# Up-projection of an MLP as seven half-size block products, and the layer's first half run for all tokens ahead of it

## The chip, the cores and the metric

The kernel runs on one core of a Trainium2 chip. The metric is the device time of one execution in microseconds (us). The kernel before has a median of 2953.45 us in 3 runs (2952.11 to 2954.23).

The engines, by the names that the profile uses: PE is TensorE (matmuls; PEld its weight loads), DVE is VectorE, ACT is ScalarE, POOL is GpSimd, SP is SyncE, whose queue issues all of this kernel's data transfers. SBUF is the on-chip memory of 128 partitions; PSUM holds the matmul results in 8 banks of 128x512 float32.

## The reference, cut to what matters

One decoder layer on 2048 tokens of width 1024, float32. What stands ahead of the last part (attention of two kinds, gates, merge) is not touched by the change and gives `mix`, 2048 x 1024. Then:

```python
x = x + mix @ w_out                                  # output projection, 1024 x 1024
h2 = rmsnorm(x, ln2_g)                               # second norm
x = x + jnp.square(jax.nn.relu(h2 @ w_up)) @ w_down  # MLP, 1024 -> 4096 -> 1024
```

## The kernel before, in words

**Precision.** Matmuls are in a reduced float32 form (`fp32r`). So every operand is split into a high part (a cast on ScalarE, line 91) and a low part (source minus high part, a subtraction on VectorE or GpSimd, line 92), and every product is three matmuls, high x high, high x low, low x high, that add up in one PSUM bank (`mm3`, lines 94 to 98). Here "a matmul" is one of these: a 128x128 stationary piece against 512 columns.

**Stages.** Attention and gates first, up to about 1353 us; they write `mix` to DRAM. Then the tokens go in two halves of 1024, `hf` = 0 and 1 (line 824), and each half passes two stages:

- Output projection, 8 blocks `i` of 128 tokens. `load_mix` loads and splits a block of `mix` and loads the same rows of x into a tile `x2[i]`; 2 x 8 products of 3 matmuls with w_out (all 16 pieces `wo` are in SBUF, in the pool "w") give `po`, which VectorE adds to `x2[i]`. Then the second norm: `norm2_pre` (a sum of squares on ScalarE, two small steps on GpSimd, a scaling `hn` on VectorE, line 758), and `norm2_post` (8 transposes `h2ps` on TensorE, a multiplication by the gain, and the split into `h2`, which stays in SBUF). `norm2_post` of a block is written behind the matmuls of the next one; that of the last block of a half behind the first unit of the MLP (line 849).
- MLP, 16 blocks `f` of 256 hidden columns. The weights of a block are loaded into the buffers `raw` (three of 4 KB a partition for all of the kernel) and split by ScalarE and GpSimd (`mlp_weights`). The up part: for two groups `c` of 512 tokens and two pieces `m` of 128 hidden columns, `up_unit` does 8 products, 24 matmuls, into one bank `pup`, then relu on ScalarE (line 820), times itself on VectorE (line 821), and the split into `u`. The down part: for 8 blocks of tokens and two halves of the width, 6 matmuls into a bank `pd`, which VectorE adds to `x2[i]` (line 860). After the last block the rows go out.

**What sets the order.** The text above is in the order in which the program writes it. The library puts it into another one at build time (`schedule_with_timeline_sim=True`, line 882): a planner takes instructions by their place in the text, but lets a later one go first on an engine where the earlier one is not ready by the planner's own estimate, or finds no free buffer. Each engine, and SP's queue of transfers, then runs its own list strictly in that order. A tile named with a `tag` takes one of `bufs` buffers, and waits for one where all are in use.

Of the kernel before, what the change touches and what calls it, by code (L numbers as in the profile page):

```python
# [43 lines left out]
RIGHT = "right"  # L44
# [15 lines left out]
def hybrid_layer(tc, x, positions, ln1_g, w_in, q_norm_a, k_norm_a, q_norm_b, k_norm_b, sinks,  # L60
                 w_branch_a, w_branch_b, w_out, ln2_g, w_up, w_down, out):
    nc = tc.nc
    x, out = x[0], out[0]
    positions = positions[0]
    w_in, w_branch_a, w_branch_b = w_in[0], w_branch_a[0], w_branch_b[0]
    w_out, w_up, w_down = w_out[0], w_up[0], w_down[0]

    const = tc.alloc_tile_pool(name="const", bufs=1)
    rawp = tc.alloc_tile_pool(name="rawp", bufs=3)
# [4 lines left out]
    edge = tc.alloc_tile_pool(name="edge", bufs=1, side=RIGHT)  # L74
# [19 lines left out]
    def mm3(out, lhs, rhs, first, last):  # L94

        nc.tensor.matmul(out, lhs[0], rhs[0], start=first, stop=False)  # L96
        nc.tensor.matmul(out, lhs[0], rhs[1], start=False, stop=False)  # L97
        nc.tensor.matmul(out, lhs[1], rhs[0], start=False, stop=last)  # L98


    ident = const.tile([P, P], F32, name="ident")
# [484 lines left out]
    pools = {}  # L586
# [5 lines left out]
    def B4(name, dtype=F32R):  # L592
        return pools["B"].tile([P, D], dtype, tag="B", bufs=19, name=name)

    def tmp(name, dtype=F32, shape=(P, 512)):
        return pools["A"].tile(list(shape), dtype, tag="tmp", bufs=4, name=name)

    def wslot(name):
        return pools["w"].tile([P, D], F32R, tag="w", bufs=16, name=name)

    def split_raw(name, r, n=D, eng=None):

        hi, lo = wslot(name + "h"), wslot(name + "l")
        split(hi[:, 0:n], lo[:, 0:n], r[:, 0:n], eng)
        return hi, lo
# [51 lines left out]
    for t in range(NBL + 5):  # L657
        if 0 < t < NBL - 1:
            a_split(t + 1)
        if t < NBL:  # L660
            a_project(t)
            g, n = blocks[t]
# [43 lines left out]
        m = t - (3 * NB + 5)  # L706
# [38 lines left out]
                    load_os(c + 2, i2)  # L745


    up_src = w_up.rearrange("(k p) n -> p k n", p=P)
    MF = FC // P
    NF = DFF // FC  # L750
    x2, h2, hn = {}, {}, {}
    mpool = pools["A"]

    def norm2_pre(i):
        xt = x2[i]
        rs = rms_scale(xt, tmp(f"junky{i}", BF16, (P, D)), mpool, i, "y")
        hn[i] = B4(f"hn{i}", F32)
        nc.vector.tensor_scalar(hn[i], xt, rs, None, op0=ALU.mult)

    def norm2_post(i):  # L760
        c = i // 4
        if i % 4 == 0:
            al = [[A4 if c % 2 == 0 or k2 == 0 else B4 for k2 in range(4)] for e in range(2)]
            h2[c] = [[al[e][k2](f"h2{e}_{c}_{k2}").rearrange("p (k t) -> p k t", k=2) for k2 in range(4)]
                     for e in range(2)]
        xt = hn.pop(i)
        pts = []
        for half in range(2):
            pt = bank(f"h2ps{i}_{half}")
            for j in range(4):  # L770
                k = 4 * half + j
                nc.tensor.transpose(pt[:, j * P:(j + 1) * P], xt[:, k * P:(k + 1) * P], ident)
            pts.append(pt)
        for half, pt in enumerate(pts):
# [4 lines left out]
            for k2 in range(2):  # L779
                hi, lo = [h2[c][e][2 * half + k2][:, :, (i % 4) * P:(i % 4 + 1) * P] for e in range(2)]  # L780
                split(hi, lo, t2[:, 2 * k2:2 * k2 + 2, :])

    def out_weights(hf):
        res = []
        for k in range(KD):
            r = raw(f"rwo{hf}_{k}")
            nc.sync.dma_start(r, w_out[k * P:(k + 1) * P, :])
            res.append(split_raw(f"wo{hf}_{k}", r, eng=nc.gpsimd if k % 2 else nc.vector))
        return res

    def mlp_weights(hf, f):
        wu, wd = [], []
        for m in range(MF):
            c0 = f * FC + m * P
            r = raw(f"rwu{hf}_{f}_{m}")
            nc.sync.dma_start(r.rearrange("p (k n) -> p k n", k=KD), up_src[:, :, c0:c0 + P])
            w = split_raw(f"wu{hf}_{f}_{m}", r, eng=nc.gpsimd)
            wu.append([[w_[:, k * P:(k + 1) * P] for w_ in w] for k in range(KD)])
        for m in range(MF):
            c0 = f * FC + m * P  # L800
            r = raw(f"rwd{hf}_{f}_{m}")
            nc.sync.dma_start(r, w_down[c0:c0 + P, :])
            wd.append(split_raw(f"wd{hf}_{f}_{m}", r, eng=nc.gpsimd))
        return wu, wd

    def load_mix(i):
        r = raw(f"rmix{i}")
        nc.sync.dma_start(r.rearrange("p (k t) -> p k t", k=KD), mix_dram[:, :, i * P:(i + 1) * P])
        mx = B4(f"mh{i}"), B4(f"ml{i}")
        split(mx[0], mx[1], r)  # L810
        x2[i] = B4(f"x2_{i}", F32)
        nc.sync.dma_start(x2[i], x[i * P:(i + 1) * P, :])
        return mx

    def up_unit(f, c, m, wu, us):
        pu = bank(f"pup{f}_{c}_{m}")
        for k in range(KD):
            mm3(pu, wu[m][k], [h2[c][e][k // 2][:, k % 2, :] for e in range(2)], k == 0, k == KD - 1)
        r = tmp(f"relu{f}_{c}_{m}")
        nc.scalar.activation(r, pu, AF.Relu)  # L820
        nc.vector.tensor_tensor(r, r, pu, op=ALU.mult)  # L821
        split(us[0][:, m * 512:(m + 1) * 512], us[1][:, m * 512:(m + 1) * 512], r)

    for hf in range(2):
        wo = out_weights(hf)
        mx = load_mix(8 * hf)
        for i in range(8 * hf, 8 * hf + 8):
            nxt = load_mix(i + 1) if i % 8 < 7 else None
            for nh in range(2):
                ns = slice(nh * 512, (nh + 1) * 512)  # L830
                po = bank(f"po{i}_{nh}")
                for k in range(KD):
                    ks = slice(k * P, (k + 1) * P)
                    mm3(po, [t[:, ks] for t in mx], [t[:, ns] for t in wo[k]], k == 0, k == KD - 1)
                nc.vector.tensor_tensor(x2[i][:, ns], x2[i][:, ns], po, op=ALU.add)
            if i % 8 > 0:
                norm2_post(i - 1)
            norm2_pre(i)
            mx = nxt
        w_next = mlp_weights(hf, 0)  # L840
        for f in range(NF):
            wu, wd = w_next
            us = {}
            for c in (2 * hf, 2 * hf + 1):
                us[c] = [B4(f"u{e}_{f}_{c}") for e in "hl"]
                for m in range(MF):
                    up_unit(f, c, m, wu, us[c])
                    if f == 0 and c % 2 == 0 and m == 0:
                        norm2_post(8 * hf + 7)
                if c == 2 * hf and f + 1 < NF:  # L850
                    w_next = mlp_weights(hf, f + 1)
            for i in range(8 * hf, 8 * hf + 8):
                u = us[i // 4]
                for nh in range(2):
                    ns = slice(nh * 512, (nh + 1) * 512)
                    pd = bank(f"pd{f}_{i}_{nh}")
                    for m in range(MF):
                        t0 = m * 512 + (i % 4) * P
# [4 lines left out]
    for pool in (pools["B"], edge, pools["A"], pools["w"], dram, psp, rawp, const):  # L863
        pool.release()


# [19 lines left out]
```

## Time and profile before

| what | us |
|---|---|
| median of 3 runs | 2953.45 |
| the profiled execution | 2951.59 |
| its span (first to last instruction) | 2949.8 |
| attention and gates, until the first output projection | 1353.9 |
| first half: first up matmul to the second half's first `po` matmul | 1447.3 to 2150.2 |
| second half: first up matmul to the last down matmul | 2243.4 to 2945.6 |

The span is the time from the first to the last instruction on the chip; what lies between it and the time of the execution is start and end. A row of the timeline gives the start, the duration, engine, source line, operation, the tile written and those read, and the count; in brackets how long the engine was idle before it and what ended that. Neighbouring matmuls overlap, so their durations add up to more than the time that passes.

### The profile page before, as it was taken

What the parts mean: (1) busy time and instruction counts of PE and PEld (TensorE: products, weight loads), DVE (VectorE), ACT (ScalarE), POOL (GpSimd) and SP (SyncE); (2) the same over time, 40 slices, a digit from 0 to 9 for tenths busy, and PEclk for the clock granted to TensorE, in tenths of its full rate; (3) what the DMA queues carried; (4) which work ended last, traced back from release to release, by engine and by line L of the source; (5) the groups of instructions that cost most, each with busy time, mean ns of one, the idle gap of its engine ahead of it and who ended that gap; (6) DMA issues with size and microseconds to landing.
All of it is one profiled execution on the core that took longest, in us unless ns stands there. A gap on an engine that the chain in (4) does not pass through costs nothing.

```text
span 2949.8 us, 37614 instructions
## 1 busy us (share of the span) xinstructions
PE 2896.2 (98%) x14665; PEld 2425.5 (82%) x14665; DVE 1415.4 (48%) x2839; ACT 1032.3 (35%) x2123; POOL 956.5 (32%) x832
## 2 busy tenths in 40 slices
PE   7999999999989999999999999999999999999999
PEld 6888888887868888888788888888887888888887
DVE  8776676569983123123543334334445344334334
ACT  5565666667873123112311211212223211211210
POOL 6566666666641102111321221212113221211210
PEclk9999999999999999999999999999999999999999
DMA  5321010011144224223311111111243111111101
GB/s 163 96 83 33 12 55 14 12 57 54 56 123 148 77 78 150 64 74 115 93 54 47 51 50 44 56 44 43 76 146 93 51 50 43 51 50 43 58 22 58
DMA packets 220259, 198.04 MB, mean 67 GB/s; under 512 B 12192, under 2 KB 189360, under 8 KB 220080
## 3 DMA queue, kind: packets, MB, share of 16 engines
q1 hardware_dynamic: 220080, 195.63, 21.6%
q8 instruction: 115, 1.88, 0.3%
q14 instruction: 64, 0.52, 0.1%
HBM read 157.65 MB, written 37.95 MB: 66 GB/s over the span
## 4 chain that ended last, share of the span: by engine, by line
PE 93%; DVE 3%; POOL 1%; ACT 1%; issue 1%; DMA 1%; SPq 0%; POOLq 0%; ACTq 0%; DVEq 0%
PE pd L97 8%; PE pd L98 8%; PE pd L96 8%; PE pup L96 8%; PE pup L97 8%; PE pup L98 8%; PE pg L98 4%; PE pg L96 4%; PE pg L97 4%; PE psA L96 3%; PE psA L98 3%; PE psA L97 3%; PE sp L416 2%; PE pt L461 2%; PE po L96 2%; PE po L97 2%
## 5 line engine op out<-in xcount | busy, mean ns | idle before, releaser
L860 DVE TENSOR_TENSOR x<-x,pd 128x512 f32<-128x512 f32 x512 | 351.4, 687 | 362.3 <-PE pd L98 358.6
L821 DVE TENSOR_TENSOR relu<-relu,pup 128x512 f32<-128x512 f32 x128 | 87.8, 686 | 393.9 <-ACT relu L820 393.9
L92 POOL TENSOR_TENSOR wd_0l<-rwd,wd_0h 128x1024 fp32r<-128x1024 f32 x32 | 76.9, 2402 | 520.5 <-ACT wd_0h L91 520.4
L96 PE MATMUL psA<-wah,hsh 128*128 128x512 f32 x512 | 208.7, 408 | 3.4 <-DVE mx L420 1.5
L97 PE MATMUL psA<-wal,hsh 128*128 128x512 f32 x512 | 202.1, 395 | 5.8 <-DVE wal L92 5.7
L91 ACT CAST wd_0h<-rwd 128x1024 fp32r<-128x1024 f32 x32 | 33.7, 1052 | 491.6 <-PE pd L97 491.6
L98 PE MATMUL psA<-wah,hsl 128*128 128x512 f32 x512 | 201.5, 394 | 1.2 <-DVE hsl L92 1.2
L96 PE MATMUL pup<-h,wu_1h 128*128 128x512 f32 x512 | 200.2, 391 | 0.0
L97 PE MATMUL pup<-h,wu_1h 128*128 128x512 f32 x512 | 199.7, 390 | 0.0
L98 PE MATMUL pup<-h,wu_1l 128*128 128x512 f32 x512 | 199.5, 390 | 0.0
L96 PE MATMUL pup<-h,wu_0h 128*128 128x512 f32 x512 | 199.3, 389 | 0.0
L97 PE MATMUL pup<-h,wu_0h 128*128 128x512 f32 x512 | 199.2, 389 | 0.0
L98 PE MATMUL pup<-h,wu_0l 128*128 128x512 f32 x512 | 199.2, 389 | 0.0
L96 PE MATMUL pd<-wd_0h,uh 128*128 128x512 f32 x512 | 199.2, 389 | 0.0
L97 PE MATMUL pd<-wd_0l,uh 128*128 128x512 f32 x512 | 199.2, 389 | 0.0
L98 PE MATMUL pd<-wd_0h,ul 128*128 128x512 f32 x512 | 199.2, 389 | 0.0
L96 PE MATMUL pd<-wd_1h,uh 128*128 128x512 f32 x512 | 199.2, 389 | 0.0
L97 PE MATMUL pd<-wd_1l,uh 128*128 128x512 f32 x512 | 199.2, 389 | 0.0
L98 PE MATMUL pd<-wd_1h,ul 128*128 128x512 f32 x512 | 199.2, 389 | 0.0
L92 POOL TENSOR_TENSOR wu_0l<-rwu,wu_0h 128x1024 fp32r<-128x1024 f32 x32 | 77.1, 2409 | 344.8 <-ACT wu_0h L91 344.8
L820 ACT ACTIVATE relu<-pup 128x512 f32<-128x512 f32 x128 | 75.7, 591 | 277.1 <-PE pup L98 277.1
L97 PE MATMUL psB<-wal,hsh 128*128 128x256 f32 x512 | 144.9, 283 | 0.0
(458 smaller groups left out, 7207.8 us busy)
## 6 DMA issues: line engine op xcount, KB each, us to landing
rwu<-in_w_up_dram SPq DMA_DIRECT2D x64, 512.0 KB, 3.9
rwd<-in_w_down_dram SPq DMA_DIRECT2D x64, 512.0 KB, 3.6
x<-in_x_dram SPq DMA_DIRECT2D x32, 512.0 KB, 4.6
rg<-in_w_in_dram SPq DMA_DIRECT2D x32, 512.0 KB, 3.7
rw<-in_w_in_dram SPq DMA_DIRECT2D x28, 384.0 KB, 3.5
hT_dram<-hT SPq DMA_DIRECT2D x16, 512.0 KB, 3.9
mix_dram<-sig SPq DMA_DIRECT2D x32, 256.0 KB, 2.0
rwo<-in_w_out_dram SPq DMA_DIRECT2D x16, 512.0 KB, 3.5
```

The costliest lines, as they stand in the source:

```text
L91: nc.scalar.copy(hi, src)
L92: (eng or nc.vector).tensor_tensor(lo, src, hi, op=ALU.subtract)
L96: nc.tensor.matmul(out, lhs[0], rhs[0], start=first, stop=False)
L97: nc.tensor.matmul(out, lhs[0], rhs[1], start=False, stop=False)
L98: nc.tensor.matmul(out, lhs[1], rhs[0], start=False, stop=last)
L416: nc.tensor.matmul(sp[:, e * 256:e * 256 + nk], ring[:, own, q_, :], ring[:, slots, k_, :], start=(i == 0), stop=(i == 1))
L461: nc.tensor.transpose(pt[:, h * P:(h + 1) * P], p[4 * q4 + h][:, kb * P:(kb + 1) * P], ident)
L820: nc.scalar.activation(r, pu, AF.Relu)
L821: nc.vector.tensor_tensor(r, r, pu, op=ALU.mult)
L860: nc.vector.tensor_tensor(x2[i][:, ns], x2[i][:, ns], pd, op=ALU.add)
```

## The change

The up-projection is computed by Strassen's algorithm, in the form of Winograd with seven products. A block of the transposed result, 256 hidden columns x 1024 tokens, is cut in 2 x 2: `A11, A21, A12, A22` are the weights (two halves of 512 input channels, two pieces of 128 hidden columns), `B11 ... B22` the activations (two halves of the input channels, two groups of 512 tokens). Four sums of weight blocks (`S1` to `S4`) and four of activation blocks (`T1` to `T4`) are formed in float32 and split. Then seven products of 4 x 3 matmuls take the place of four units of 8 x 3. In the order of the text, and called P1 to P7 below: A11 B11, S1 T1, S2 T2, A12 B21, S3 T3, A22 T4, S4 B22. Four PSUM banks collect them; P4, P5 and P7 add into a bank that holds an earlier product, after that one has been read. VectorE combines the banks into the four quarters of the result (`c11`, `u3`, `c22`, `u2`) in SBUF.

The order of the stages changes too. The output projection and the second norm now run for all 16 blocks of tokens in one go, w_out is loaded and split once, and x2 and h2 are stored to DRAM. Then the pools of these stages are released, and new ones lie over their space, each tile of which waits for the old tiles at its place (`reuse_waits="tile"`). For each half, `token_operands` loads h2 through the `raw` buffers, four k slices of two loads each, and makes the seven activation operands, which stay in SBUF for the half's 16 blocks (14 tiles of 8 KB; there is one set). `x2` is loaded again. The weight operands of a block have 10 tiles where one block uses 14; the split w_down has 4, one block's worth. The sums of the weights and all their splits are on GpSimd and ScalarE. The scratch area for transfers that GpSimd would issue is cut to 256 bytes.

```diff
-    def up_unit(f, c, m, wu, us):
-        pu = bank(f"pup{f}_{c}_{m}")
-        for k in range(KD):
-            mm3(pu, wu[m][k], [h2[c][e][k // 2][:, k % 2, :] for e in range(2)], k == 0, k == KD - 1)
-        r = tmp(f"relu{f}_{c}_{m}")
-        nc.scalar.activation(r, pu, AF.Relu)
-        nc.vector.tensor_tensor(r, r, pu, op=ALU.mult)
-        split(us[0][:, m * 512:(m + 1) * 512], us[1][:, m * 512:(m + 1) * 512], r)
...
+    mx = load_mix(0)
+    for i in range(NB):
+        nxt = load_mix(i + 1) if i + 1 < NB else None
...
+        nc.sync.dma_start(x2_dram[i * P:(i + 1) * P, :], x2[i])
+        if i > 0:
+            norm2_post(i - 1)
+        norm2_pre(i)
+        mx = nxt
+    norm2_post(NB - 1)
+    for pool in (pools["B"], pools["A"], pools["w"]):
+        pool.release()
...
+    def token_operands(hf):
+
+        ops = {n: [poolT.tile([P, 4, 512], F32R, tag="t", bufs=14, name=f"{n}{e}{hf}") for e in "hl"]
+               for n in B_NAMES}
+        ts = slice(1024 * hf, 1024 * hf + 1024)
+        for k in range(4):
+            r1, r2 = raw(f"rh1_{hf}_{k}"), raw(f"rh2_{hf}_{k}")
+            nc.sync.dma_start(r1, h2_dram[:, k, ts])
+            nc.sync.dma_start(r2, h2_dram[:, k + 4, ts])
+            b11, b12, b21, b22 = r1[:, 0:512], r1[:, 512:1024], r2[:, 0:512], r2[:, 512:1024]
+
+            def put(n, src, eng):
+                split(ops[n][0][:, k, :], ops[n][1][:, k, :], src, eng)
+
+            put("B11", b11, nc.vector)
+            t1, t2 = Ft(f"t1_{hf}_{k}"), Ft(f"t2_{hf}_{k}")
+            nc.gpsimd.tensor_tensor(t1, b12, b11, op=ALU.subtract)
+            put("T1", t1, nc.vector)
+            nc.vector.tensor_tensor(t2, b22, t1, op=ALU.subtract)
+            put("T2", t2, nc.vector)
+            put("B21", b21, nc.gpsimd)
+            t3, t4 = Ft(f"t3_{hf}_{k}"), Ft(f"t4_{hf}_{k}")
+            nc.gpsimd.tensor_tensor(t3, b22, b12, op=ALU.subtract)
+            put("T3", t3, nc.vector)
+            nc.vector.tensor_tensor(t4, b21, t2, op=ALU.subtract)
+            put("T4", t4, nc.vector)
+            put("B22", b22, nc.gpsimd)
+        return ops
+
+    def up_operands(hf, f):
+
+        r = []
+        for h in range(2):
+            r.append(raw(f"rwu{hf}_{f}_{h}").rearrange("p (k n) -> p k n", k=4))
+            nc.sync.dma_start(r[h], up_src[h][:, :, f * FC:(f + 1) * FC])
...
+        def summed(n, a, b, op):
+            t = poolS.tile([P, 4, P], F32, tag="s", bufs=2, name=f"s{n}_{hf}_{f}")
+            nc.gpsimd.tensor_tensor(t, a, b, op=op)
+            return t
...
+        def put(n, src):
+            res[n] = [poolS.tile([P, 4, P], F32R, tag="S", bufs=10, name=f"{n}{e}_{hf}_{f}") for e in "hl"]
+            split(res[n][0], res[n][1], src, nc.gpsimd)
+
+        put("A11", a11)
+        s1 = summed("1", a21, a22, ALU.add)
+        put("S1", s1)
+        s2 = summed("2", s1, a11, ALU.subtract)
+        put("S2", s2)
+        put("A12", a12)
+        s4 = summed("4", a12, s2, ALU.subtract)
+        s3 = summed("3", a11, a21, ALU.subtract)
+        put("S3", s3)
+        put("A22", a22)
+        put("S4", s4)
+        return res
...
+        def done(src, m, c):
+
+            nc.vector.scalar_tensor_tensor(src, src, 0.0, src, op0=ALU.max, op1=ALU.mult)
+            split(us[c][0][:, m * 512:(m + 1) * 512], us[c][1][:, m * 512:(m + 1) * 512], src)
...
+        product(ba, "A11", "B11")
+        nc.scalar.copy(p1, ba)
+        product(bc, "S1", "T1")
+        product(bb, "S2", "T2")
+        nc.vector.tensor_tensor(u2, p1, bb, op=ALU.add)
+        product(ba, "A12", "B21", more=True)
+        c11 = Ft(f"fc11_{tag}")
+        nc.scalar.activation(c11, ba, AF.Relu)
+        nc.vector.tensor_tensor(c11, c11, ba, op=ALU.mult)
+        split(us[0][0][:, 0:512], us[0][1][:, 0:512], c11)
+        product(bb, "S3", "T3", more=True)
+        nc.vector.tensor_tensor(u3, p1, bb, op=ALU.add)
+        nc.vector.tensor_tensor(c22, u3, bc, op=ALU.add)
+        product(bd, "A22", "T4")
+        nc.vector.tensor_tensor(u3, u3, bd, op=ALU.add)
+        done(u3, 1, 0)
+        done(c22, 1, 1)
+        product(bc, "S4", "B22", more=True)
+        nc.vector.tensor_tensor(u2, u2, bc, op=ALU.add)
+        done(u2, 0, 1)
+        return us
 
     for hf in range(2):
...
+        A_next = up_operands(hf, 0)
+        B = token_operands(hf)
+        for j in range(8):
+            i = 8 * hf + j
+            x2[i] = poolX.tile([P, D], F32, tag="x2", bufs=8, name=f"x2m_{i}")
+            nc.sync.dma_start(x2[i], x2_dram[i * P:(i + 1) * P, :])
         for f in range(NF):
...
+            A = A_next
+            us = up_products(hf, f, A, B)
+            wd = down_operands(hf, f)
+            if f + 1 < NF:
+                A_next = up_operands(hf, f + 1)
```

## Rows read from the trace of the kernel before

**Rows 1.** The page's first part: busy us, share of the span, instructions.

```profile
span 2949.8 us, 37614 instructions
PE 2896.2 (98%) x14665; PEld 2425.5 (82%) x14665; DVE 1415.4 (48%) x2839; ACT 1032.3 (35%) x2123; POOL 956.5 (32%) x832
```

**Rows 2.** TensorE's waits from 1340 us on: us in total, times, longest.

```profile
PE h2ps L772 <- DVE hn L758: 7.3, 2, 3.7
```

**Rows 3.** Windows, one MLP block: PE, PEld, DVE, ACT, POOL, clock, DMA, GB/s.

```profile
1600.00:1643.52 43.52, 43.52 (x193) 36.05 (x192) 16.79 (x24) 8.77 (x12) 9.56 (x4) 1.00 0.16 49
```

**Rows 4.** The page's groups: busy us, mean ns of one, idle before.

```profile
L96 PE MATMUL pd<-wd_0h,uh 128*128 128x512 f32 x512 | 199.2, 389 | 0.0
```

**Rows 5.** TensorE's timeline within an up part: start us, duration us.

```profile
1600.71 0.39 PE L96 MATMUL pup<-h,wu_1h 128*128 128x512 f32 x1
1600.93 0.39 PE L97 MATMUL pup<-h,wu_1h 128*128 128x512 f32 x1
```

**Rows 6.** TensorE's timeline at the handovers and at the end.

```profile
1447.33 0.48 PE L96 MATMUL pup<-h,wu_0h 128*128 128x512 f32 x1
...
1456.68 1.91 PE L772 MATMUL h2ps<-ident,hn 128*128 128x128 f32 x8 [3.65 <-DVE hn L758]
1458.24 0.78 PE L96 MATMUL pup<-h,wu_1h 128*128 128x512 f32 x1
1458.82 0.63 PE L97 MATMUL pup<-h,wu_1h 128*128 128x512 f32 x1
...
2150.15 0.39 PE L96 MATMUL po<-wo_0h,mh 128*128 128x512 f32 x1
...
2243.36 0.48 PE L96 MATMUL pup<-h,wu_0h 128*128 128x512 f32 x1
...
2945.64 0.39 PE L98 MATMUL pd<-wd_1h,ul 128*128 128x512 f32 x1
```

**Rows 7.** Windows, after TensorE's wait in the first handover; the clock is 0.73.

```profile
1457.00:1463.00 6.00, 6.00 (x25) 5.12 (x24) 5.28 (x5) 3.76 (x7) 5.95 (x3) 0.73 0.61 188
```

**Rows 8.** Groups by form in the MLP, the last from the page.

```profile
L860 DVE TENSOR_TENSOR x<-x,pd 128x512 f32<-128x512 f32 x512 | 351.4, 687 | 362.3 <-PE pd L98 358.6
L92 DVE TENSOR_TENSOR ul<-relu,uh 128x512 fp32r<-128x512 f32 x128 | 104.8, 819 | 64.6 <-ACT uh L91 64.6
...
L91 ACT CAST uh<-relu 128x512 fp32r<-128x512 f32 x128 | 79.5, 621 | 115.2 <-DVE relu L821 115.2
...
L92 POOL TENSOR_TENSOR wd_0l<-rwd,wd_0h 128x1024 fp32r<-128x1024 f32 x32 | 76.9, 2402 | 520.5 <-ACT wd_0h L91 520.4
```

**Rows 9.** Timelines of VectorE and GpSimd, alone and side by side.

```profile
1597.53 0.69 DVE L92 TENSOR_TENSOR ul<-relu,uh 128x512 fp32r<-128x512 f32 x1 [0.69 <-ACT uh L91]
...
1601.85 2.40 POOL L92 TENSOR_TENSOR wu_0l<-rwu,wu_0h 128x1024 fp32r<-128x1024 f32 x1 [12.25 <-ACT wu_0h L91]
...
1603.67 1.13 DVE L92 TENSOR_TENSOR ul<-relu,uh 128x512 fp32r<-128x512 f32 x1 [0.69 <-ACT uh L91]
...
1438.19 0.75 DVE L758 TENSOR_SCALAR hn<-x,rsxy 128x1024 f32<-128x1024 f32 x1
...
1453.59 2.48 POOL L92 TENSOR_TENSOR wu_0l<-rwu,wu_0h 128x1024 fp32r<-128x1024 f32 x1
1456.03 2.82 POOL L92 TENSOR_TENSOR wu_1l<-rwu,wu_1h 128x1024 fp32r<-128x1024 f32 x1
...
1453.79 2.83 DVE L758 TENSOR_SCALAR hn<-x,rsxy 128x1024 f32<-128x1024 f32 x1
1456.54 0.68 DVE L821 TENSOR_TENSOR relu<-relu,pup 128x512 f32<-128x512 f32 x1
```

**Rows 10.** SP's timeline ahead of the second handover.

```profile
2201.48 0.38 SPq L796 DMA_DIRECT2D rwu<-in_w_up_dram  x1
```

**Rows 11.** ScalarE's timeline in the last output projection of the first half.

```profile
1441.75 1.05 ACT L91 CAST wu_0h<-rwu 128x1024 fp32r<-128x1024 f32 x1 [3.55 <-PE po L97]
```

**Rows 12.** The page's DMA issues: count, KB each, us from issue to landing.

```profile
rwu<-in_w_up_dram SPq DMA_DIRECT2D x64, 512.0 KB, 3.9
```

More of the change, by code (lines that the diff above doesn't have):

```diff
@@ L92, in split, with mm3 @@
         (eng or nc.vector).tensor_tensor(lo, src, hi, op=ALU.subtract)
[L94 to L98, printed above, removed]
+    def mm3(out, lhs, rhs, first, last, more=False):
+        nc.tensor.matmul(out, lhs[0], rhs[0], start=first, stop=False, skip_group_check=more)
+        nc.tensor.matmul(out, lhs[0], rhs[1], start=False, stop=False, skip_group_check=more)
+        nc.tensor.matmul(out, lhs[1], rhs[0], start=False, stop=last, skip_group_check=more)
     ident = const.tile([P, P], F32, name="ident")
@@ L760, in norm2_post @@
     def norm2_post(i):
[L761 to L765, printed above, removed]
         xt = hn.pop(i)
-        pts = []
         for half in range(2):
@@ L778, in norm2_post @@
                                     g2T[:, ks].unsqueeze(2).broadcast_to([P, 4, P]), op=ALU.mult)
[L779 to L784, printed above, removed]
-        for k in range(KD):
[L786 to L804, printed above, removed]
+            nc.sync.dma_start(h2_dram[:, ks, i * P:(i + 1) * P], t2)
     def load_mix(i):
@@ new lines, in hybrid_layer @@
+    wo = []
+    for k in range(KD):
+        r = raw(f"rwo{k}")
+        nc.sync.dma_start(r, w_out[k * P:(k + 1) * P, :])
+        wo.append(split_raw(f"wo{k}", r, eng=nc.gpsimd if k % 2 else nc.vector))
+    mx = load_mix(0)
+    for i in range(NB):
+        nxt = load_mix(i + 1) if i + 1 < NB else None
+        for nh in range(2):
+            ns = slice(nh * 512, (nh + 1) * 512)
+            po = bank(f"po{i}_{nh}")
+            for k in range(KD):
+                ks = slice(k * P, (k + 1) * P)
+                mm3(po, [t[:, ks] for t in mx], [t[:, ns] for t in wo[k]], k == 0, k == KD - 1)
+            nc.vector.tensor_tensor(x2[i][:, ns], x2[i][:, ns], po, op=ALU.add)
+        nc.sync.dma_start(x2_dram[i * P:(i + 1) * P, :], x2[i])
[3 more added lines that the diff above has]
+        mx = nxt
@@ new lines, in hybrid_layer, with Ft @@
+    poolS, poolD, poolF, poolT, poolX = SP
+    up_src = w_up.rearrange("(h k p) n -> h p k n", p=P, h=2)
+    B_NAMES = ("B11", "T1", "T2", "B21", "T3", "T4", "B22")
+    A_NAMES = ("A11", "S1", "S2", "A12", "S3", "A22", "S4")
+    def Ft(name):
+        return poolF.tile([P, 512], F32, tag="f", bufs=5, name=name)
+    def token_operands(hf):
[23 more added lines that the diff above has]
+        return ops
@@ new lines, in down_operands, with up_products, product @@
+    def down_operands(hf, f):
+        res = []
+        for m in range(MF):
+            r = raw(f"rwd{hf}_{f}_{m}")
+            nc.sync.dma_start(r, w_down[f * FC + m * P:f * FC + (m + 1) * P, :])
+            w = [poolD.tile([P, D], F32R, tag="d", bufs=4, name=f"wd{e}_{hf}_{f}_{m}") for e in "hl"]
+            split(w[0], w[1], r, nc.gpsimd)
+            res.append(w)
+        return res
+    def up_products(hf, f, A, B):
+        us = [[poolX.tile([P, D], F32R, tag="u", bufs=4, name=f"u{e}_{hf}_{f}_{c}") for e in "hl"]
+              for c in range(2)]
+        def product(ps, a, b, more=False):
+            for k in range(4):
+                mm3(ps, [t[:, k, :] for t in A[a]], [t[:, k, :] for t in B[b]],
+                    k == 0 and not more, k == 3, more)
+        def done(src, m, c):
+            nc.vector.scalar_tensor_tensor(src, src, 0.0, src, op0=ALU.max, op1=ALU.mult)
+            split(us[c][0][:, m * 512:(m + 1) * 512], us[c][1][:, m * 512:(m + 1) * 512], src)
+        tag = f"{hf}_{f}"
+        ba, bb, bc, bd = [bank(f"p{n}{tag}") for n in "abcd"]
+        p1, u2, u3, c22 = [Ft(f"{n}_{tag}") for n in ("fp1", "fu2", "fu3", "fc22")]
+        product(ba, "A11", "B11")
[19 more added lines that the diff above has]
+        return us
@@ L862, in hybrid_layer @@
                         nc.sync.dma_start(out[i * P:(i + 1) * P, ns], x2[i][:, ns])
-    for pool in (pools["B"], edge, pools["A"], pools["w"], dram, psp, rawp, const):
+    for pool in (poolX, poolT, edge, poolF, poolD, poolS, dram, psp, rawp, const):
         pool.release()
```

54 lines of the change are left out of this document (17 added, 37 removed).

## The prediction

> **What bounds the kernel now.** I read the page's busy times first: TensorE is busy in 98% of the span [rows 1]. Then TensorE's waits over the last 1600 us, the output projections and the MLP: two, 7.3 us in all, both for the last norm of a half [rows 2]. Then one MLP block (256 hidden columns for 1024 tokens: 96 up and 96 down matmuls): 43.52 us with TensorE busy throughout, VectorE 16.8, ScalarE 8.8, GpSimd 9.6 [rows 3]. So the MLP is bound by the number of matmuls, and a removed one is worth its time on TensorE, as long as nothing new is late.
>
> What one matmul is worth must be read from starts, not from durations. The groups show 389 ns for a 128x512 matmul [rows 4]; two neighbours start 0.22 to 0.23 us apart [rows 5], and 43.52/192 = 0.2267 us. The Trainium skill, Perfetto Trace Analysis, Identifying the Most-Contended Engine, warns that matmul busy time is no good measure because matmuls are pipelined; by the 389 ns the change would give back 149 us, by the spacing 87. The trace bears the page out, and the sum uses 0.2267.
>
> **What the change removes.** Per block seven products of 12 matmuls (84) take the place of four units of 24 (96). There are 32 blocks: 384 x 0.2267 = 87.0 us. A block becomes 180 x 0.2267 = 40.8: up 19.04 (2.72 a product, P1 to P7), down 21.76.
>
> The two handovers from a half's output projection to its MLP go as well. A half runs from 1447.33 to 2150.15 and from 2243.36 to 2945.87 (the last matmul's start plus one spacing) [rows 6], 702.8 and 702.5 us against 3072 x 0.2267 = 696.3: a surplus of 12.7 in all. It is TensorE waiting 3.65 us for hn, the transposes, and matmuls that start 0.58 apart after that, with a mean granted clock of 0.73 over 1457 to 1463, so part of it at the 1.2 GHz level [rows 6, 7]. What new gaps cost is counted below from the packed 40.8. Removed: 99.7 us.
>
> **What a block adds, and what hides it.** GpSimd: 4 sums and 7 low-part subtractions of 128x512, and two of 128x1024 for w_down. The 128x1024 takes 2.40 us [rows 8], a half-size one so 1.2: 11 x 1.2 + 4.8 = 18.0 of 40.8 us (now 9.6). VectorE: 22 operations with a PSUM operand at 0.687 (16 are the down additions) and 7 with both inputs in SBUF, of which the relu-square has no row in that form (at least the 0.55 us left of a blocked subtraction, below, at most the mean 0.82 of `ul`; I take 0.69): 20 us. ScalarE: eleven 128x512 casts at 0.62, two of 128x1024, a copy and a relu, about 10. Loads stay at 2 MB. No engine comes near 40.8, so only chains can cost.
>
> Within the up part: p1 is copied out of its bank by 4.2 us (P4 overwrites it at 8.16), u2 reads its bank by 9.1 (P5 at 10.88), c22 by 15.3 to 16.0 (P7 at 16.32). Zero, with little to spare at the last. The w_down pieces have only one set of tiles, free when the previous down part ends; ScalarE and GpSimd need 6 to 9 of the 19 us for them. The ten S tiles (of 14 needed) free one pair per product, so GpSimd's operands for the next block run from about 9 to 21 us, and need be ready at 40.8. Both zero; without that cover up to 9 us a block.
>
> The tight chain is the second half of the first tokens' u, which the down part's second three matmuls read. P6 ends at 16.32, its result 0.16 later (0.39 less the spacing); then the addition 0.69, the relu-square 0.69, the cast 0.62, the subtraction 0.69 and some 0.3 of hand-offs (an estimate): 19.5. The low part is wanted by the sixth down matmul, 19.04 + 5 x 0.2267 = 20.17. Slack 0.7 us.
>
> Against it stands what the trace shows of VectorE and GpSimd: a subtraction (`ul`) of 0.69 us took 1.13 when it started inside GpSimd's 1601.85 to 1604.25, ending 0.55 after it; hn, otherwise 0.75, took 2.83 under GpSimd's operation that began 0.2 us earlier; a multiplication with a PSUM operand started in the next GpSimd operation and took 0.68 as always [rows 9]. So an operation with both inputs in SBUF waits for GpSimd's running one. Two of the chain's four steps are of that kind, each can wait up to 1.2 us, and GpSimd is in its dense stretch just then. Bounds for the stall, s, per block: 0 (GpSimd idle there) to 2 x 1.2 + 0.8 (another relu-square queued between them) - 0.7 = 2.5. Followed through, GpSimd's s3 ends near 18.15, the chain's subtraction near 21.1: 0.9, which I take. For the 31 blocks that prepare a successor within their half or the next: 28 us.
>
> The Trainium skill, SBUF - State Buffer, Who interferes with whom, makes of this a rule: a VectorE instruction with two SBUF inputs and a GpSimd instruction that reads SBUF exclude each other for a whole instruction, and issue order decides who blocks. The rows above agree. Applied to both steps at its worst it speaks against this change: 31 x 2.5 = 78 us; that is rival C.
>
> **The first handover (F1).** The new half needs all of B11 (four k slices) before P1 ends. The build's planner issues loads early: rwu at 2201, 42 us before its use at 2243 [rows 6, 10]. So two weight pieces and the first h2 slice fill the three raw buffers in time; the second h2 slice then waits for the first weight piece. That one is held until s3 is formed, and the S and s tiles lie over w_out's, which come free only in the last pass: now too wu's first cast waits for a po matmul, at 1441.75 [rows 11]. From the last po matmul: 8 GpSimd operations x 1.2 and the last norm's two small steps (1.0, an estimate), 10.6 us, then a load of 3.9 [rows 12], 14.6 with rounding. The second weight piece stays until A22, hence until P1 is through: the other h2 slices go through two buffers. Per slice GpSimd and VectorE take turns: t2, t4, T2 at 0.62 (0.69 less overlap), t3, B21, B22 at 1.2: 5.5, plus 0.4 issue and 3.9 load: 9.8. Twice that, then 1.9 + 0.4 + 3.9 for the last first-half slice and 1.9 for its B11: 27.7. P1 ends 0.7 later, 43.0 instead of 2.7: F1 = 40. The slow clock after the gap (2 us, from rows 6) and parts of P2, P3 and P6 done early (up to 3) I set off against each other. Bounds: 14 if the operands come as fast as the last norm's own chain (first up matmul to those transposes, 1447.33 to 1456.68, is 9.4, plus P1's operands and the clock); 68 if every load (4.3) and its work (7 x 0.62 + 4 x 1.2 = 9.1) follow each other: 14.6 + 4 x 13.4.
>
> **The second handover (F2).** The same 28.4 us, started when the first weight piece is given back in the last block: GpSimd's s3 at about 22, the load at 26.3; P1 ends at 54.7 where 43.5 would be packed: 11. The 16 additions of the last down part share VectorE (11 of its 22 us): 3 more. F2 = 14; bounds 0 (all prepared under the down part) and 40 (nothing before its end).
>
> **The rest.** One pass over w_out less: its loads and splits are hidden now and give nothing. Stores and reloads of x2 and h2 add 33 MB, a store of 1 MB a block on SP's queue beside loads issued a block ahead; between 0 and 1 us a block, 0 taken. The smaller scratch area serves transfers of GpSimd's, of which there are none. The transposes of block 7 cost 0.8 in the new place, below the rounding.
>
> **Sum.** 2949.8 - 99.7 + 40 + 14 + 28 = 2932. The profiled execution took 2951.6, 1.8 over its span, and the median of the runs is 1.9 above that: 2936 in the median's terms.
>
> **Rivals.**
> - B, the handovers are covered: F1 14, F2 2, s 0.3 (9 us): 2949.8 - 99.7 + 25 + 3.7 = 2879. For it: the planner's early loads and the absence of waits in every MLP block. Against: three raw buffers, one of them held until P1 is over.
> - C, slower, by the lock of VectorE and GpSimd at the start of every down part: s = 2.5, 78 us, with F as in the forecast: 2949.8 - 99.7 + 54 + 78 + 3.7 = 2986. It turns the sign at s = (99.7 - 54)/31 = 1.5 us. For it: hn lost 2.1 us to that lock [rows 9], so the order was not planned around it. Against: TensorE's queue may have other down matmuls ahead.
> - D, the handovers are serial: F1 68, F2 35, s 0.9: 2949.8 - 99.7 + 131 + 3.7 = 2985. For it: nothing of the new pools can start before w_out is done. Against: B11 does not need the sums, and its tiles lie over others.
> - That the matmuls saved are not on the path: ruled out by rows 2 and 3.
>
> **Chances.** Forecast 0.50, B 0.22, C 0.18, D 0.10. What can be told from no change is about 0.2%, 6 us. The forecast's own range is 2905 to 2965; of its half, 0.40 lies below 2947.5, 0.07 within, 0.03 above. B is all faster; C gives 0.03 to no change and 0.15 to slower; D 0.02 and 0.08. Faster 0.62, same 0.12, slower 0.26. The range for 8 in 10 takes in most of B, and of C and D the nearer part: 2882 to 2990.
>
> **What would show it.** 2688 up matmuls at 0.2267 apart; blocks of 40.8 us plus s, the idle time ahead of a `pd` matmul that waits for VectorE's `ul`; one gap of some 40 us (whole or in pieces, waiting for B11, T or for raw loads) after the last `po`, one of some 14 near the MLP's middle. Blocks of 43 us or more would make C right; gaps under 10 us, B; a period clearly above 0.2267 within a product would upset the whole sum.

## The result and the profile after

| what | before, us | after, us |
|---|---|---|
| median of 4 runs each, side by side | 2952.78 (2951.19 to 2954.23) | 2913.44 (2911.47 to 2914.77) |
| the profiled execution, its span | 2951.59, 2949.8 | 2914.77, 2912.7 |
| last `po` matmul's end to last `pd` matmul's end | | 1366.8 |

The ratio is 0.9866, with a 95% interval of 0.9849 to 0.9883: 39.3 us faster, where 17.5 were forecast. The time lies inside the stated range of 2882 to 2990.

The page's first part after, as in [rows 1] (busy us, share of the span, instructions), and its group that answers to [rows 4]:

```profile
span 2912.7 us, 37930 instructions
PE 2827.6 (97%) x14281; PEld 2358.1 (81%) x14281; DVE 1598.6 (55%) x2987; ACT 1069.4 (37%) x2203; POOL 1314.8 (45%) x1148
...
L96 PE MATMUL pd<-wdh,uh 128*128 128x512 f32 x1024 | 398.7, 389 | 0.9 <-ACT uh L91 0.7
```

14665 - 14281 = 384 TensorE instructions are gone, as counted. The group still shows 389 ns for one matmul and hardly any idle time ahead of the down matmuls.

TensorE's waits from 1300 us on in the kernel after (us in total, times, longest), to be read against the one line of [rows 2]:

```profile
PE pa L96 <- ACT B11h L91: 14.8, 4, 6.6
PE pb L97 <- DVE T2l L92: 7.0, 4, 1.9
PE h2ps L765 <- DVE hn L757: 6.6, 1, 6.6
PE pb L96 <- ACT T2h L91: 3.6, 4, 1.6
PE pa L97 <- DVE B11l L92: 3.2, 5, 1.2
PE pc L97 <- DVE T1l L92: 1.7, 1, 1.7
PE pd L96 <- ACT uh L91: 0.7, 1, 0.7
PE pd L98 <- DVE ul L92: 0.5, 1, 0.5
```

The waits are for operands of the tokens (B11, T1, T2) and for the last norm. The wait that the forecast made most of, a `pd` matmul for VectorE's `ul`, is the last line: once, 0.5 us.

Windows of the kernel after: first handover, a block of the first half, second handover, and 14 blocks of the second half (columns as in [rows 3]):

```profile
1542.00:1626.00 84.00, 56.09 (x197) 40.32 (x196) 62.34 (x62) 29.30 (x50) 58.42 (x39) 0.72 0.44 150
...
2156.58:2197.38 40.80, 40.80 (x181) 33.78 (x180) 21.54 (x29) 9.84 (x16) 19.44 (x13) 1.00 0.16 52
2238.00:2297.00 59.00, 49.12 (x189) 36.96 (x188) 46.31 (x54) 19.84 (x34) 38.28 (x23) 0.86 0.53 194
2296.70:2867.90 571.20, 571.20 (x2521) 472.97 (x2520) 305.50 (x406) 137.64 (x211) 272.14 (x182) 1.00 0.17 52
```

Away from the handovers TensorE is busy throughout, and a block takes exactly 40.80 us (571.20/14), 180 matmuls at 0.2267. So s, the stall per block, is 0. Everything above the packed 32 x 40.8 = 1305.6 is at the two handovers: 1366.8 - 1305.6 = 61.2 us. The first is F1 = 43.5: block f = 1 of the first half (its first matmul of P1) starts at 1626.18, and packed behind the last `po` matmul (its start plus one spacing, 1541.89) it would start at 1541.89 + 40.8 = 1582.69. The second is F2 = 17.7: from the start of the first half's last block (2197.38) to that of the second half's block f = 1 (2296.70) pass two blocks' 81.6 us and 17.7 more. These two stand below for each kernel, worked out in the same way.

### The profile page after: what moved, and what is told of

The parts are those of the page before. It is cut to its first block, busy times and chain, and to the rows that moved or that the text cites. A ratio compares the mean times of both kernels' runs of the same rounds, so it can differ in the third digit from the quotient of the medians.

```text
span 2912.7 us, 37930 instructions
## 1 busy us (share of the span) xinstructions
PE 2827.6 (97%) x14281; PEld 2358.1 (81%) x14281; DVE 1598.6 (55%) x2987; ACT 1069.4 (37%) x2203; POOL 1314.8 (45%) x1148
## 3 DMA queue, kind: packets, MB, share of 16 engines
q1 hardware_dynamic: 209968, 225.00, 24.6%
## 4 chain that ended last, share of the span: by engine, by line
PE 90%; DVE 5%; DMA 2%; POOL 1%; issue 1%; ACT 1%; SPq 0%; POOLq 0%; DVEq 0%; ACTq 0%
PE pd L96 9%; PE pd L97 9%; PE pd L98 9%; PE pg L96 4%; PE pg L98 4%; PE pg L97 4%; PE psA L96 4%; PE psA L97 3%; PE psA L98 3%; PE pb L96 3%; PE pb L97 3%; PE pb L98 3%; PE sp L416 2%; PE pt L461 2%; PE po L97 2%; PE po L96 2%
## 5 line engine op out<-in xcount | busy, mean ns | idle before, releaser
L962 DVE TENSOR_TENSOR x2m<-x2m,pd 128x512 f32<-128x512 f32 x512 | 328.6, 682 | 135.7 <-PE pd L98 135.7
L96 PE MATMUL pd<-wdh,uh 128*128 128x512 f32 x1024 | 398.7, 389 | 0.9 <-ACT uh L91 0.7
L97 PE MATMUL pd<-wdl,uh 128*128 128x512 f32 x1024 | 398.4, 389 | 0.0
L92 POOL TENSOR_TENSOR wdl<-rwd,wdh 128x1024 fp32r<-128x1024 f32 x64 | 152.4, 2405 | 468.1 <-ACT wdh L91 468.1
L98 PE MATMUL pd<-wdh,ul 128*128 128x512 f32 x1024 | 362.1, 389 | 0.5 <-DVE ul L92 0.5
L96 PEld LDWEIGHTS pd<-wdh,uh 128*128 128x128 f32 x1024 | 192.2, 188 | 42.0 <-ACT uh L91 1.7
L98 PEld LDWEIGHTS pd<-wdh,ul 128*128 128x128 f32 x1024 | 192.2, 188 | 40.8 <-DVE ul L92 0.9
L97 PEld LDWEIGHTS pd<-wdl,uh 128*128 128x128 f32 x1024 | 192.2, 188 | 39.9
L312 DVE TENSOR_REDUCE hss<-sq 128x8 f32<-128x512 f32 x64 | 43.8, 685 | 186.3 <-ACT sq L311 186.2
L98 PE MATMUL psB<-wah,hsl 128*128 128x256 f32 x512 | 145.3, 284 | 0.0
L96 PE MATMUL psB<-wah,hsh 128*128 128x256 f32 x512 | 143.9, 281 | 0.0
```

The costliest lines, as they stand in the source:

```text
L312: nc.vector.tensor_reduce(ss[:, 0:8], sq, axis=AX, op=ALU.add)
```

## Why no block stalled: the order of TensorE's queue

One block end in the kernel after (the block starts at 2115.78). TensorE's timeline: start us, duration, line, operation:

```profile
2131.88 0.39 PE L98 MATMUL pd<-T4h,A22l 128*128 128x512 f32 x1
2132.10 0.39 PE L96 MATMUL pd<-wdh,uh 128*128 128x512 f32 x1
...
2134.37 1.30 PE L98 MATMUL pd<-wdh,ul 128*128 128x512 f32 x5
...
2135.96 0.39 PE L98 MATMUL pd<-wdh,ul 128*128 128x512 f32 x1
2136.18 0.39 PE L96 MATMUL pc<-B22h,S4h 128*128 128x512 f32 x1
...
2138.90 0.39 PE L96 MATMUL pd<-wdh,uh 128*128 128x512 f32 x1
```

VectorE's and GpSimd's in the same stretch:

```profile
2133.59 0.69 DVE L933 TENSOR_TENSOR fu<-fu,pd 128x512 f32<-128x512 f32 x1
2134.20 0.86 DVE L913 SCALAR_TENSOR_TENSOR fc<-fc 128x512 f32<-128x512 f32 x1
2134.98 1.78 DVE L913 SCALAR_TENSOR_TENSOR fu<-fu 128x512 f32<-128x512 f32 x1
2136.68 0.68 DVE L92 TENSOR_TENSOR ul<-fc,uh 128x512 fp32r<-128x512 f32 x1
2137.45 0.69 DVE L92 TENSOR_TENSOR ul<-fu,uh 128x512 fp32r<-128x512 f32 x1
```

```profile
2133.22 1.29 POOL L92 TENSOR_TENSOR A12l<-rwu,A12h 128x512 fp32r<-128x512 f32 x1
2134.47 1.73 POOL L869 TENSOR_TENSOR s<-rwu 128x512 f32<-128x512 f32 x1
```

The lock that the forecast feared is there: the relu-square of `fu` took 1.78 us beside GpSimd's sum. The low part is ready at 2138.14, 22.36 us into the block; in the written order it would be wanted at 20.17. But TensorE does not run the written order. Between P6's last matmul (2131.88) and P7's first (2136.18) stand 18 down matmuls, six banks' share of the first hidden half, whose `u` comes from `c11` and had long been ready. They move P7 4.1 us back, and no down matmul behind P7 starts before 2138.90, when the late low part is ready. The planner put them there at build time.

Theory: the chain is late in every block, and this order alone hides it. Rival: the chain would be in time in the written order too (the forecast's slack, or VectorE's order). Two experiments tell them apart. In the diffs from here on, comments are added and long lines end in `...`.

**The written order.** From block f = 1 on, each of TensorE's MLP matmuls is held behind the one written before it, an order within one queue that adds no wait between engines:

```diff
+            if chain["on"]:                     # f > 0
+                if chain["last"] is not None:
+                    tc.add_manual_dep(ins.ins, chain["last"].name, ...)
+                chain["last"] = ins.ins
```

> From the second block of each half on, TensorE's matmuls are held to the order of the text: P7 and then the down part, instead of 18 down matmuls of the first hidden half put in front of P7. Theory (the queue's order, not a spare GpSimd, took away the stall at the start of the down part): the low part of the chain's u, which in the changed kernel is ready 22.4 us into a block, is now wanted at 20.2; each of 30 blocks gets 1.5 to 2.5 us longer (42.3 to 43.3 instead of 40.8), and the span grows by 45 to 75 us, to 2958 to 2988. Rival 1 (VectorE and GpSimd hardly meet on this chain): under 0.3 us a block, span below 2922. Rival 2 (my forecast's 0.9 us): 27 us, 2940.

Measured: 3014.32 us in one run, span 3012.3, 99.6 over the kernel after and slower than the kernel before. The 28 block steps away from the handovers are 43.3 to 45.6 us, 44.4 in the mean: s = 3.6. TensorE's waits in this kernel from 1300 us on, the first of them (all matmuls have line 99 here), one block end on TensorE and VectorE (the block starts at 1847.95), and windows behind the same wait in an earlier block and in this one:

```profile
PE pd L99 <- DVE ul L92: 59.3, 30, 3.6
```

```profile
1868.33 0.40 PE L99 MATMUL pd<-wdl,uh 128*128 128x512 f32 x1
1870.70 0.50 PE L99 MATMUL pd<-wdh,ul 128*128 128x512 f32 x1 [1.98 <-DVE ul L92]
```

```profile
1863.97 1.61 DVE L919 SCALAR_TENSOR_TENSOR fc<-fc 128x512 f32<-128x512 f32 x1
1865.50 0.67 DVE L939 TENSOR_TENSOR fu<-fu,pd 128x512 f32<-128x512 f32 x1
1866.21 1.08 DVE L919 SCALAR_TENSOR_TENSOR fu<-fu 128x512 f32<-128x512 f32 x1
1867.21 1.77 DVE L92 TENSOR_TENSOR ul<-fc,uh 128x512 fp32r<-128x512 f32 x1
1868.90 1.74 DVE L92 TENSOR_TENSOR ul<-fu,uh 128x512 fp32r<-128x512 f32 x1
```

```profile
1648.40:1651.30 2.90, 2.90 (x8) 2.31 (x7) 2.32 (x4) 0.62 (x1) 0.00 (x0) 0.50 0.00 0
1870.70:1873.00 2.30, 2.30 (x10) 1.89 (x11) 2.18 (x4) 0.62 (x1) 0.00 (x0) 1.00 0.00 0
```

The wait falls on the matmul that the forecast named, the sixth of the down part. Four VectorE operations with both inputs in SBUF are blocked here, 1.08 to 1.77 us each instead of 0.69. The low part is ready at 1870.64, 22.7 us into the block, nearly as in the kernel after (22.4): what changed is when it is wanted.

The 59.3 us of named waits are not all of the 99.6. From start to start of neighbouring matmuls, over the 0.2267 spacing, the 28 blocks lose 2.5 us each at the fourth to sixth down matmul, where `uh` and `ul` are waited for, 0.1 ahead of them, and 1.0 in the mean behind them, where nothing is waited for. That last part is 1.5 to 1.8 us in 15 of the blocks and under 0.2 in the other 13. In the 15 the matmuls behind the wait start 0.43 us apart for a while: the granted clock is 0.50 from 1648.40 to 1651.30, the 1.2 GHz level, after TensorE had stood for 2 us. Behind an equal wait at 1870.70 it stays at 1.00; what decides between the two is not shown. So the chain alone costs 2.5 us a block, the upper end of the expectation, which had no term for the clock. The last block of the second half, with no successor whose weights GpSimd would prepare, took 41.12 us from its first up matmul to the last down matmul's start, against 40.57 in the kernel after.

**The written order with GpSimd quiet.** The same order, and from f = 1 on GpSimd makes neither the sums nor the low parts of the up weights (the kernel leaves out the sums and the low parts; ScalarE's copies of the plain blocks stand in their place):

```diff
+            if f > 0:
+                return a                        # summed(): no sum
...
+            if f > 0:
+                nc.scalar.copy(res[n][0], src)
+                nc.scalar.copy(res[n][1], src)
```

> The order of the text as in e1, and GpSimd has almost nothing to do beside the chain: from the second block of each half on the four weight sums are left out (a plain block stands for each) and the weights' low parts are copies made by ScalarE. Left out of the computation: those sums and low parts. Theory (the stall in e1 is VectorE waiting for GpSimd's running operation): without it the chain takes 19.5 us and is wanted at 20.2, so blocks are back at 40.8 to 41.1, span 2905 to 2922. Rival (the written order is late by itself, whatever GpSimd does): as in e1, 42.3 us and more a block, span above 2955.

Measured: 2919.64 us in one run, every block away from the handovers 40.80 us, and no TensorE wait at all from 1630 to 2190 us. F1 is 45.1 and F2 18.9, 2.8 more than after, and that is most of the 5 us of its span. VectorE's relu-squares of `fu` take 0.69 us in the median there. So the stall in the written order is GpSimd's work beside VectorE's, and without it the written order would do.

## What the seven products are worth by themselves

The changed kernel with eight plain products in place of the seven: the same stages, pools and loads, but B11 to B22 by A11 to A22, 96 up matmuls a block, no sums or differences:

```diff
-B_NAMES = ("B11", "T1", "T2", "B21", "T3", "T4", "B22")
+B_NAMES = ("B11", "B12", "B21", "B22")
...
+        for m, c in ((0, 0), (1, 0), (0, 1), (1, 1)):
+            ps = bank(f"p{m}{c}{tag}")
+            for h in range(2):                  # 2 x 4 x 3 matmuls into one bank
```

> The order of the stages and the pools of the changed kernel, but eight plain products (B11, B12, B21, B22 by A11, A12, A21, A22, each 12 matmuls) in place of the seven: 96 up matmuls a block. Theory (the number of TensorE's matmuls is the whole gain of the products, 0.2267 us each): blocks of 43.5 us, +87 us for the 32 blocks, less some 5 to 15 because a slice of h2 now needs 4 low parts and no sums: 2985 to 3000 us, slower than the kernel before, which had no gaps of this size at its handovers. Rival (the new order of the stages brings a good part of the gain): 2940 to 2955.

Measured: 2963.28 us in one run, span 2961.5. That is between the two expectations. Blocks are 43.52 as the theory has them, but the gaps shrink further than I expected: F1 24.6 instead of 43.5, F2 0 instead of 17.7. Its waits from 1300 us on:

```profile
PE p L96 <- ACT B11h L91: 9.3, 2, 4.7
PE h2ps L765 <- DVE hn L757: 5.4, 1, 5.4
```

So the change splits in two. The new order of the stages alone costs 2963.3 - 2953.0 = 10 us. The seven products take 32 x 2.72 = 87.0 us off the blocks and put 61.2 - 24.6 = 36.6 back at the handovers, where eleven operations a slice take the place of four and the weights' sums are added: 50 net.

## What sets the handovers

Three suspects for the first: the reloads of `x2` ahead of the second h2 slice, the raw buffers (one of three is held by the second weight piece until A22), and VectorE and GpSimd taking turns. SP's queue in the kernel after, then the first matmul of P1's second k slice, and VectorE with the second slice:

```profile
1553.18 0.33 SPq L837 DMA_DIRECT2D rh<-h_dram  x1
1553.60 4.86 SPq L947 DMA_DIRECT2D x2m<-x_dram  x8
1559.99 0.32 SPq L836 DMA_DIRECT2D rh<-h_dram  x1
```

```profile
1570.11 0.79 PE L96 MATMUL pa<-B11h,A11h 128*128 128x512 f32 x1 [6.64 <-ACT B11h L91]
```

```profile
1570.09 1.21 DVE L92 TENSOR_TENSOR B11l<-rh,B11h 128x512 fp32r<-128x512 f32 x1 [5.61 <-ACT B11h L91]
1571.22 1.77 DVE L847 TENSOR_TENSOR t<-rh,t 128x512 f32<-128x512 f32 x1
1572.91 1.75 DVE L92 TENSOR_TENSOR T1l<-t,T1h 128x512 fp32r<-128x512 f32 x1
1574.58 1.75 DVE L853 TENSOR_TENSOR t<-rh,t 128x512 f32<-128x512 f32 x1
1576.26 1.76 DVE L92 TENSOR_TENSOR T2l<-t,T2h 128x512 fp32r<-128x512 f32 x1
```

The slice issued at 1559.99 is used by GpSimd at 1569.48, so its load took 9.4 us behind 4 MB of `x2m`; the median of the first half's eight loads is 3.6. And four VectorE operations in a row take 1.75 to 1.77 us where an unblocked one takes 0.69. Each suspect was taken away alone, in pairs, and all together.

**x2 reloads written later** (behind the first block's `down_operands`; the move alone, no order forced):

> The eight reloads of x2 (4 MB a half) stand behind the first block's products instead of ahead of them. Theory for the first gap's 43.5 us: they are queued ahead of the second h2 slice, whose load took 9.4 us from issue instead of 3.6; without them the first gap shrinks by 5 to 6 us, the second by 1 to 2 (there they were spread out): span 2904 to 2907. Rival (only the three buffers set the pace of the slices): no change beyond 1 us, 2912. Second rival: they now hold up the w_down loads of the first block, and the gain is lost again in the first down part, 2911 to 2916.

Measured: 2914.12 us (2911.62 to 2916.11). Miss, and no test: SP's queue still issues the eight `x2m` ahead of the second slice, from 1551.90 on, as nothing keeps the planner from it, and the wait of 6.6 us stands. The place in the text did not decide the order.

**x2 reloads held behind the h2 slices and the first w_down pieces** on SP's queue, first half only:

```diff
+                if behind is not None:          # the last w_down load of f = 0
+                    tc.add_manual_dep(ld.ins, behind.name, ...)
```

> The eight reloads of x2 (4 MB) of the first half are held behind the h2 slices and the first w_down pieces on SP's queue. Theory (in the changed kernel the second h2 slice landed 9.4 us after its issue because 4 MB were queued ahead of it, against 3.6 for such a load alone): it lands 4 to 6 us earlier, TensorE's wait of 6.6 us for B11h shrinks to 1 to 2, and the time is 4 to 6 us below the changed kernel's (2907 to 2910). Rival (VectorE and GpSimd, which take turns at the operands, set the pace, the load is hidden by them): 0 to 2 us below.

Measured: 2910.06 us (2908.81 to 2913.04), F1 40.2. 3.4 us below the kernel after, between the two expectations. P1's first matmuls of the four slices in this kernel:

```profile
1553.91 0.80 PE L96 MATMUL pa<-B11h,A11h 128*128 128x512 f32 x1 [3.81 <-ACT B11h L91]
1561.57 0.80 PE L96 MATMUL pa<-B11h,A11h 128*128 128x512 f32 x1 [0.67 <-ACT B11h L91]
1573.35 0.80 PE L96 MATMUL pa<-B11h,A11h 128*128 128x512 f32 x1 [0.58 <-ACT B11h L91]
1582.19 0.79 PE L96 MATMUL pa<-B11h,A11h 128*128 128x512 f32 x1 [0.73 <-ACT B11h L91]
```

The wait of 6.64 us is 0.67 now, so the 4 MB were its cause. From the last `po` matmul's start (1541.66 after, 1540.27 here) the second slice is 7.2 us earlier than in the kernel after, the third 4.4, the fourth 3.0 (there 1570.11, 1579.09, 1586.54): more than half of the lead is lost again.

**Second weight piece loaded twice**, so that its first buffer is free before A22 is formed (f = 0 of both halves):

```diff
+            if f == 0:
+                late = raw(f"rwv{hf}")[:, 0:512].rearrange("p (k n) -> p k n", k=4)
+                nc.sync.dma_start(late, up_src[1][:, :, P:2 * P])
+            put("A22", late)
```

> For the first block of a half the piece A22 is loaded a second time, behind the h2 slices, so that the second weight buffer is given back before P1 ends. Theory (the h2 slices go through two of the three buffers): with three the slices come 1.5 to 3 us closer together, each gap shrinks by 4 to 8 us, span 2897 to 2905. Rival (VectorE and GpSimd, taking turns for 8 to 9 us a slice, set the pace): under 2 us in all, 2910 to 2914, or 1 to 2 us longer for A22 comes later.

Measured: 2911.93 us (2911.32 to 2912.86), F1 42.4, F2 16.7: 1.5 us, the theory of buffers alone missed.

**Token operands on VectorE alone**: in `token_operands` the four `nc.gpsimd` become `nc.vector`.

> The four operations of each h2 slice that GpSimd did (two differences, two low parts) go to VectorE, in both halves. Theory (taking turns sets the slices' pace: VectorE's subtractions took 1.64 to 1.78 us there instead of 0.68): eleven operations at 0.62 are 6.8 us a slice instead of 8.5 to 9.5, and the time is 3 to 9 us below the changed kernel's. Rival (the raw buffers and loads set the pace, or GpSimd's operations were in parallel after all): a slice takes 6.8 + 4 us, and the time is 0 to 6 us above the changed kernel's.

Measured: 2915.38 us (2914.62 to 2916.43), F1 43.8, F2 17.9. No gain, the rival's side, although VectorE's operations of the first three slices take 0.68 or 0.69 us each now: VectorE idles 6.57 us until the second slice's load is in. In the fourth slice, from 1586.90 on, four of them are blocked again, 1.77 to 2.90 us each, beside GpSimd's low parts of the weights.

**The pairs.**

> The pair of the x2 loads behind and the token operands on VectorE, without the second load of the weight piece. Theory (three things in series at the first handover: a slice's load, two raw buffers instead of three, the operands' operations; whichever is left paces it): two buffers pace, a load of some 4 us does not lie beside the operands of the slice before, 4 slices lose 1 to 2 us each: 2903 to 2907. Rival (the weight piece's second load gives nothing, as when it was tried alone): 2899 to 2901, as all three.

> The pair of the x2 loads behind and the second load of the weight piece; the operands are shared by VectorE and GpSimd as in the changed kernel. Theory (as for the other pairs): the taking of turns paces, 8.5 us a slice: 2906 to 2909. Rival (the operands' sharing costs nothing): 2899 to 2902.

> The pair of the token operands on VectorE and the second load of the weight piece; the x2 loads go ahead of the second h2 slice as in the changed kernel. Theory (as for the other pairs): the second slice is 5 to 6 us late, VectorE idles for it: 2904 to 2908. Rival (the 4 MB ahead of it cost nothing with three buffers): 2899 to 2901.

**All three.**

> The reloads of x2 behind the h2 slices, the token operands on VectorE alone, and a second load of the second weight piece that sets a raw buffer free, all three. If the first handover is a chain of load, VectorE and buffers, each of which gives its part: 43.5 us becomes 30 to 36, and the time is 2899 to 2907 us. If one of them sets the pace and the others are hidden by it: no better than the best of the three alone, 2906 to 2912.

| kernel | median us | F1 | F2 |
|---|---|---|---|
| after | 2913.4 | 43.5 | 17.7 |
| x2 behind | 2910.1 | 40.2 | 17.3 |
| second load | 2911.9 | 42.4 | 16.7 |
| operands on VectorE | 2915.4 | 43.8 | 17.9 |
| x2 behind, operands | 2910.6 | 39.8 | 18.4 |
| x2 behind, second load | 2909.2 | 40.0 | 16.3 |
| operands, second load | 2907.9 | 42.2 | 13.5 |
| all three | 2899.9 | 36.0 | 12.1 |

Each alone gives -1.9 to +3.4 us, a pair 2.9 to 5.6, all three 13.5 (2898.91 to 2901.36; ratio to the kernel before 0.9823, interval 0.9809 to 0.9836). The interval of each ratio reaches some 4 us to either side, so the single edits are not clear of noise by their times; F1 + F2 of the traces, one execution each, give the same order: 61.2 after, 57.5 to 61.7 for one edit, 55.7 to 58.2 for two, 48.1 for all three. The first pair missed its range (2903 to 2907): with two buffers VectorE, faster now, waits for each slice's load, 0.5 to 2.5 us at a time. The others fell within or 0.2 us outside theirs. This is the best version that was run. Its VectorE in the first handover, the first and the last rows:

```profile
1554.43 0.69 DVE L847 TENSOR_TENSOR t<-rh,t 128x512 f32<-128x512 f32 x1 [0.71 <-DMA rh<-h_dram]
1555.04 0.69 DVE L92 TENSOR_TENSOR T1l<-t,T1h 128x512 fp32r<-128x512 f32 x1
...
1578.86 0.68 DVE L92 TENSOR_TENSOR T3l<-t,T3h 128x512 fp32r<-128x512 f32 x1
1579.46 0.68 DVE L92 TENSOR_TENSOR T4l<-t,T4h 128x512 fp32r<-128x512 f32 x1
```

From 1553 to 1580 it runs 43 operations, nearly all 0.60 us apart, with two gaps of 0.7 and 0.2 us. Only with all three does one engine run almost without gaps; with any one missing, the loads or the taking of turns open gaps again. The expectation for it had the gains as parts that add; they do not add. The time came at the lower end of its range, F1 with 36.0 at the upper end of its 30 to 36: 5.6 of the 13.5 us are at the second handover.

## Why the prediction was off, step by step

- **Matmuls removed: right.** 384 fewer, 0.2267 us apart; blocks 40.80, 87.0 us.
- **Old handovers' surplus of 12.7: right.** With eight plain products the span is 11.7 us longer than before with a new gap of 24.6, so the old gaps came to some 13.
- **F1 = 40: near, 43.5 measured.** The first part went as worked out: the second `rh` tile of the first slice is issued at 1553.18, when the sum S3 frees the first weight piece, 11.1 us after the last `po` matmul's end (10.6 forecast). Mis-sized is the second slice's load, 9.4 us instead of 3.9: I counted the stores and reloads of `x2` as bytes over a block (0 taken), not as 4 MB ahead of one load that TensorE waits for. The view of waits and the held-back reloads (F1 40.2) show it. That F1 came so near in spite of it is in part luck: P1's four slices start 14.8, 9.0 and 7.5 us apart (1555.30 to 1586.54), where the forecast had 9.8, 9.8 and 8.1.
- **F2 = 14: near, 17.7 measured.** Which of its terms is short was not taken apart.
- **s = 0.9, 28 us: the step that failed.** It took the time at which the low part is wanted, 20.17 us into a block, from the written order. In TensorE's own queue 18 down matmuls go before P7, and s is 0. The prediction named exactly this against rival C and then did not use it for its own s. In the written order the chain costs 2.5 us a block, the upper bound and not the 0.9 that I took: four operations are blocked and not the two I followed, among them the relu-square and the low part of the other group of tokens queued between. The 3.6 us measured there have 1.0 more, for which the forecast's s had no term: matmuls at the 1.2 GHz level behind the wait. The lock is real: `hn` of [rows 9], a scaling by one number a partition, was not its best witness, but `ul` there and the rows above are. What it costs is decided by what stands in TensorE's queue.
- **The sum.** 2949.8 - 99.7 + 43.5 + 17.7 + 0 = 2911.3; the span is 2912.7, of which 1.2 is a later first `po` matmul. Against the forecast span of 2932: 28 less from s, 3.5 and 3.7 more from F1 and F2, 1.4 more for the rest.
- **Rivals.** B had s right and both handovers far too short. C's mechanism is there and turns the sign in the written order (3014 us), but only in that order. D did not come: F1 and F2 are 43.5 and 17.7, not 68 and 35. The gain would be 50 rather than 39 us if the new order of the stages cost nothing.

## What to carry to other kernels

When a chain looks tight, look for work on the consumer's engine that is ready earlier and that the planner can put ahead, before you price the wait: here 18 ready matmuls in front made 2.5 us of stall a block into none. The products saved by an algorithm that adds sums of operands were worth their matmuls in the steady state here, and the sums came due where the pipeline starts; price them there first. When loads, buffers and two engines that block each other pace a start together, taking one away shows little, and a small gain does not clear it of blame: try them together.

## What the runs showed of the hardware that was not expected

- A GpSimd operation can be the one that loses time to VectorE. In the kernel with all three edits, beside VectorE's unbroken row (GpSimd's timeline):

```profile
1575.27 6.00 POOL L92 TENSOR_TENSOR A22l<-rwv,A22h 128x512 fp32r<-128x512 f32 x1 [22.57 <-ACT A22h L91]
```

  6.00 us for an operation that otherwise takes 1.26 to 1.3; TensorE then waits 4.4 us for it. It ends 1.1 us after VectorE's last operation of the row has (1580.14). The pair without the held-back reloads has such a row too: 5.42 us from 1582.27, ending 1.1 us after VectorE's. It is no rule: with the operands on VectorE alone, the same operation started at 1586.67 within a VectorE row as close and took 1.46 us, and VectorE's next took 1.78.

  The Trainium skill, SBUF — State Buffer, Who interferes with whom, says that issue order and not the kind of operation decides who blocks. The row agrees in that GpSimd can lose as well as VectorE; but seven VectorE operations that started after 1575.27 ran ahead of GpSimd's, so the order of the starts does not tell who comes first, and what does is not shown.
- The scalar_tensor_tensor form with both inputs in SBUF is blocked as the subtraction is: up to 1.78 us beside GpSimd, a mean of 1.66 over the 64 of `fu` in the kernel after; with GpSimd quiet (the written order's second kernel) 0.69 in the median.
- In the first handover of the kernel after, TensorE runs at the 1.2 GHz level while it waits between short runs of matmuls:

```profile
1556.00:1594.00 38.00, 20.59 (x41) 11.57 (x41) 30.71 (x26) 16.73 (x30) 23.78 (x16) 0.50 0.60 218
```

  Neighbours that wait for nothing start 0.43 us apart there, and 0.23 apart after 1594.2. That is part of F1, as the forecast had it for a shorter stretch.
